# PEER gate weights built once at full width, half of them kept in DRAM; modulation rows split over two layers; one-hot sums of the MoE on VectorE

## The chip, the core and the metric

The kernel runs on one core of a Trainium2 chip. A core has TensorE for matrix multiplies (PE in the profile; its weight loads are PEld), VectorE (DVE), ScalarE (ACT), GpSimd (POOL) and SyncE (SP), which here only issues transfers. Engines run their own instructions in order and wait for each other through semaphores. SBUF is the on-chip memory of 128 partitions, PSUM the accumulators of TensorE, DRAM the large memory outside. The metric is the time of one execution in microseconds (us).

## The reference

Two transformer blocks in a row on 256 tokens of width 1024. The first has two layers of attention and a PEER feed-forward; the second has recurrent mixers and a mixture of experts (MoE) with 64 experts. The change touches three parts of it:

```python
# PEER, per token: 8 heads pick 16 of 128 x 128 experts each
top_s, pos = lax.top_k(cand, PEER_TOPK)
eidx = jnp.take_along_axis(cidx, pos, axis=-1)
g = jax.nn.softmax(top_s, axis=-1)
a = gelu(einsum('chkd,cd->chk', u[eidx], xc))
w = g * a
out = einsum('chk,chkd->cd', w, v[eidx])
...
# second block, before its layer: 6 modulation rows from a vector c
m = silu(c) @ w_mod[:, : 6 * D_MODEL] + b_mod
...
# MoE: 8 of 64 experts per token
sel = lax.top_k(cand, TOP_K)[1]
```

## The kernel before, in words

The kernel does not gather PEER's experts. It computes `u` times all tokens for all 128 x 128 experts, applies Gelu, multiplies by a dense gate array that is zero where an expert wasn't picked, and multiplies by all of `v`. `peer` does this for each layer `l` in four stages. An expert's number has two parts of 7 bits; a step `s` holds two values of the second part, each with 128 experts on the partitions.

- **First u half**, `ustep(0..31)`: each step loads two slots of `in_u` (512 KB each, tiles `rawA` and `rawB`), splits each into a high and a low part (`whi` by ACT, L280, `wlo` by DVE, L284), and runs 48 matmuls of 256 columns (three for each of 8 x 2 pieces). ACT applies Gelu into `WA`. Routing runs beside it.
- **Second u half**, `ustep(32..63)`: the same into `WB`. Beside it run 32 `gstep(g0, 0)`, one for 8 tokens each, which build the gates of `WA`.
- **First v half**, `vstep(0..31)`: each step splits two rows of `WA` into `hh` and `hl`, loads two slots of `in_v` and runs 24 matmuls of 512 columns into `acc`. Beside it run 32 `gstep(g0, 1)`, which build the gates of `WB`.
- **Second v half**, `vstep(32..61)` and `vlast`: the same on `WB`. In layer 0 there are beside it 48 `mod_step`: each loads 512 KB of `in_wmod` into the same `raw` tiles and DVE multiplies and sums it (L910).

A `gstep` makes one-hot matrices of 8 tokens by comparing with a row 0..127. `o1` (L739) compares with the first part of the expert's number, `oa` (L741) with the second part, 64 of the 128 values at a time; `ob` and `oa` are then multiplied by the low and the high part of the gate (L743, L744). The element order is (pair of token groups, value, token), with 4 tokens innermost and 16-bit elements. 16 matmuls `o1` x `oa` and `o1` x `ob` of 64 columns give the gates of 8 tokens in one PSUM tile `ps`, and DVE multiplies them into `W` (L751). So `o1` is built twice for each token, once per half. The tiles of a gstep lie in `a.raw` (`hr` in the profile), in two buffers that take turns.

`interleave(main, side)` writes the side steps between the main ones, each after the last `wlo` of the step before it (`issue_after(self.pin)`). The scheduler of the language then fixes the order on each engine. PSUM tiles alternate between tags `psA` and `psB`, two buffers each; `raw`, `whi` and `wlo` have two buffers per tag A and B, so two steps of weights are in SBUF at a time. `in_u`, `in_v` and `in_wmod` are all issued from SP, in order.

In the MoE, `onehot(q4)` builds for 4 experts two comparisons on DVE (L1643), then their sum `O` on POOL (L1644; for the first group on DVE) and its copy in bf16 `Ob` on POOL (L1645). `gather` uses `O` as the moving operand, `slots` uses `Ob`. POOL also computes the low part of every second down weight (`xlo`, L284).

Of the kernel before, what the change touches and what calls it, by code (L numbers as in the profile page):

```python
# [214 lines left out]
class K:  # L215
# [493 lines left out]
    def peer(self, l, a):  # L709
        nc, I, tc = self.nc, self.I, self.tc  # L710
        H = NK // 2
        with ExitStack() as es:
# [19 lines left out]
            def gstep(g0, hf):  # L732
                def f():
                    tk = lambda x: x[:, g0:g0 + 8].rearrange("p (g t) -> p g t", g=2).unsqueeze(2)
                    k = (g0 // 8) % 2
                    buf = a.raw[:, 4 * k:4 * k + 4, :].rearrange("p a n -> p (a n)").bitcast(F16)
                    o1 = buf[:, 0:1024].rearrange("p (g n t) -> p g n t", g=2, t=4)
                    oa, ob = [buf[:, 1024 + 512 * i:1536 + 512 * i].rearrange("p (g n t) -> p g n t", g=2, t=4) for i in range(2)]
                    nc.vector.tensor_tensor(o1, self.iota4.unsqueeze(1).broadcast_to([P, 2, 128, 4]),  # L739
                                            tk(idx[0]).broadcast_to([P, 2, 128, 4]), op=OP.is_equal)  # L740
                    nc.vector.tensor_tensor(oa, self.iota4[:, hf * H:(hf + 1) * H].unsqueeze(1).broadcast_to([P, 2, H, 4]),  # L741
                                            tk(idx[1]).broadcast_to([P, 2, H, 4]), op=OP.is_equal)
                    nc.vector.tensor_tensor(ob, oa, tk(idx[3]).broadcast_to([P, 2, H, 4]), op=OP.mult)  # L743
                    nc.vector.tensor_tensor(oa, oa, tk(idx[2]).broadcast_to([P, 2, H, 4]), op=OP.mult)  # L744
                    ps = self.ps()
                    for i in range(8):
                        o = ps[:, i * H:(i + 1) * H]
                        self.mm(o, o1[:, i // 4, :, i % 4], oa[:, i // 4, :, i % 4], i == 0, False)
                        self.mm(o, o1[:, i // 4, :, i % 4], ob[:, i // 4, :, i % 4], False, i == 7)
# [1209 lines left out]
```

## Time and profile before

| | |
|---|---|
| median of 3 runs | 3294.72 us (3287.04 to 3298.88) |
| the profiled execution | 3290.99 us |
| its span of instructions | 3289.2 us |
| PE busy | 3101.9 us, 94% |
| DVE busy | 2505.5 us, 76% |
| ACT busy | 1587.2 us, 48% |
| POOL busy | 512.5 us, 16% |
| mean DMA rate | 185 GB/s |

The difference between span and execution, 1.8 us, lies around the instructions. A busy PE is not PE at its peak: matmuls overlap, so their rate is read from the distance of their starts.

### The profile page before, as it was taken

How to read it: one execution, taken by the hardware profiler on the slowest of the kernel's cores; microseconds unless marked ns; L12 is line 12 of the kernel's file. 1: busy time of each engine (PE TensorE's matmuls, PEld its weight loads, DVE VectorE, ACT ScalarE, POOL GpSimd, SP SyncE). 2: the span in 40 equal slices, each digit the busy share in tenths (PEclk: the TensorE clock that was granted, in tenths of full speed). 3: DMA queues.
4: the chain of work that ended last, by engine and by line, in shares of the span. 5: the costliest groups of instructions: out<-in, count | busy, mean ns of one | idle time of the engine just before them, and what ended most of it. 6: DMA issues, size and time to landing. Idle time of an engine off the chain costs nothing. (4 is left out here: it accounts for less than half of the span.)

```text
span 3289.2 us, 53389 instructions
## 1 busy us (share of the span) xinstructions
PE 3101.9 (94%) x20908; PEld 2778.7 (84%) x20908; DVE 2505.5 (76%) x4367; ACT 1587.2 (48%) x2136; POOL 512.5 (16%) x278
## 2 busy tenths in 40 slices
PE   5999999999999899999999999979998899999997
PEld 5889999998876688999999888868897777877776
DVE  7655997778877776599777885566868888888886
ACT  4544443343344434444334334443244676667665
POOL 2010220000000323122000000010332332232221
PEclk8999999999999899999999999989998999999999
DMA  6335554445588521555544555642223678877875
GB/s 241 112 103 180 180 176 159 155 159 161 162 279 299 209 65 46 180 179 178 164 154 157 163 161 180 195 166 96 90 96 122 247 285 292 286 276 282 292 277 187
DMA packets 166726, 607.84 MB, mean 185 GB/s; under 512 B 18752, under 2 KB 19264, under 8 KB 165824
## 3 DMA queue, kind: packets, MB, share of 16 engines
q1 hardware_dynamic: 166464, 604.33, 54.3%
q8 instruction: 166, 2.72, 0.3%
q14 instruction: 96, 0.79, 0.1%
HBM read 600.57 MB, written 3.69 MB: 184 GB/s over the span
## 5 line engine op out<-in xcount | busy, mean ns | idle before, releaser
L280 ACT CAST whiA<-rawA 128x1024 fp32r<-128x1024 f32 (+1 forms) x439 | 460.4, 1049 | 582.3 <-PE psA L253 247.7
L280 ACT CAST whiB<-rawB 128x1024 fp32r<-128x1024 f32 (+1 forms) x449 | 471.3, 1050 | 531.6 <-PE psA L253 191.4
L284 DVE TENSOR_TENSOR wloA<-rawA,whiA 128x1024 fp32r<-128x1024 f32 x406 | 530.6, 1307 | 151.3 <-ACT whiA L280 148.4
L284 DVE TENSOR_TENSOR wloB<-rawB,whiB 128x1024 fp32r<-128x1024 f32 x421 | 528.8, 1256 | 129.6 <-ACT whiB L280 127.8
L253 PE MATMUL psA<-hh,whiA 128*128 128x256 f32 (+1 forms) x1096 | 322.2, 294 | 5.4 <-ACT hh L293 5.4
L253 PE MATMUL psA<-hl,whiA 128*128 128x256 f32 (+1 forms) x1096 | 316.4, 289 | 3.5 <-DVE hl L294 3.5
L253 PE MATMUL psA<-hh,wloA 128*128 128x256 f32 (+1 forms) x1096 | 316.0, 288 | 0.8 <-DVE wloA L284 0.7
L284 POOL TENSOR_TENSOR xlo<-xraw,xhi 128x1024 fp32r<-128x1024 f32 x64 | 164.3, 2568 | 484.4 <-ACT xhi L280 484.4
L253 PE MATMUL psA<-hh,whiB 128*128 128x256 f32 x832 | 238.1, 286 | 0.5 <-ACT hh L293 0.5
L253 PE MATMUL psA<-hl,whiB 128*128 128x256 f32 x832 | 235.4, 283 | 2.3 <-DVE hl L294 2.3
L253 PE MATMUL psA<-hh,wloB 128*128 128x256 f32 x832 | 235.4, 283 | 0.7 <-DVE wloB L284 0.7
L284 POOL TENSOR_TENSOR wloB<-rawB,whiB 128x1024 fp32r<-128x1024 f32 x28 | 74.5, 2662 | 985.3 <-ACT whiB L280 985.3
L284 POOL TENSOR_TENSOR wloA<-rawA,whiA 128x1024 fp32r<-128x1024 f32 x33 | 86.0, 2608 | 911.6 <-ACT whiA L280 846.4
L253 PEld LDWEIGHTS psA<-hh,whiA 128*128 128x128 f32 (+1 forms) x1096 | 216.2, 197 | 7.5 <-ACT hh L293 6.4
L253 PEld LDWEIGHTS psA<-hl,whiA 128*128 128x128 f32 (+1 forms) x1096 | 215.5, 197 | 5.7 <-issue 1.9
L253 PEld LDWEIGHTS psA<-hh,wloA 128*128 128x128 f32 (+1 forms) x1096 | 215.1, 196 | 1.7 <-DVE wloA L284 1.4
L253 PE MATMUL acc<-whiA,hh 128*128 128x512 f32 x512 | 199.2, 398 | 7.7 <-ACT whiA L280 5.8
L253 PE MATMUL acc<-wloA,hh 128*128 128x512 f32 x512 | 201.1, 393 | 4.9 <-DVE wloA L284 4.3
L253 PE MATMUL acc<-whiB,hh 128*128 128x512 f32 x512 | 202.2, 396 | 2.1 <-ACT hh L293 1.9
L253 PE MATMUL acc<-wloB,hh 128*128 128x512 f32 x512 | 199.8, 390 | 0.8 <-DVE wloB L284 0.8
L253 PE MATMUL acc<-whiA,hl 128*128 128x512 f32 x512 | 199.3, 390 | 0.0
L253 PE MATMUL acc<-whiB,hl 128*128 128x512 f32 x512 | 199.2, 390 | 0.0
(835 smaller groups left out, 8364.9 us busy)
## 6 DMA issues: line engine op xcount, KB each, us to landing
rawA<-in_moegu SPq DMA_DIRECT2D x130, 512.0 KB, 5.4
rawB<-in_moegu SPq DMA_DIRECT2D x130, 512.0 KB, 5.2
rawA<-in_u SPq DMA_DIRECT2D x128, 512.0 KB, 3.5
rawB<-in_u SPq DMA_DIRECT2D x128, 512.0 KB, 3.5
rawA<-in_v SPq DMA_DIRECT2D x128, 512.0 KB, 3.6
rawB<-in_v SPq DMA_DIRECT2D x128, 512.0 KB, 3.5
xraw<-in_moed SPq DMA_DIRECT2D x128, 512.0 KB, 5.8
rawB<-in_wt SPq DMA_DIRECT2D x40, 512.0 KB, 3.5
```

The lines of the kernel that those rows point to most:

```text
L253: self.pe = self.nc.tensor.matmul(out, lhsT, rhs, start=start, stop=stop, skip_group_check=True).ins
L280: self.nc.scalar.copy(hi[:, :n], w[:, :n])
L284: i = (eng or self.nc.vector).tensor_tensor(lo[:, :n], w[:, :n], hi[:, :n].bitcast(F32), op=OP.subtract)
```

## The change

- **Gates.** `gstep` now makes all 128 values of the second part at once: `oa` and `ob` are twice as wide, `o1` is built once, and a gstep has 16 matmuls of 128 columns into two PSUM tiles. So there are 32 gsteps per layer where there were 64. All of them run in the second u half, beside `ustep(32..61)`. DVE multiplies the first 64 values into `WA` at once, in two pieces. The other 64 are for rows of `WB` that Gelu hasn't written yet: ACT copies them out of PSUM (`late`), POOL writes them to a DRAM array `dgate` (256 KB per gstep), and in the first v half SP loads them back (`gload`, four ahead) and DVE multiplies them into `WB` (`gate`).
- The innermost dimension of the one-hots has 2 tokens (`iota2`) where it had 4.
- The buffers of the gsteps are `a.raw` (8 KB of it) and, for odd steps below `GT` = 28, the end of `WB`, which Gelu writes last.
- **Modulation.** 24 of the 48 `mod_step` run in the second v half of each layer.
- **One-hot sums.** `O` and `Ob` are both computed on DVE from the two comparisons; POOL has no part in `onehot`.

```diff
+GT = 28
...
-        self.iota4 = self.t(self.cp, [128, 4], "iota4", F16)
+        self.iota2 = self.t(self.cp, [128, 2], "iota2", F16)
...
-            def gstep(g0, hf):
+            def gstep(g):
                 def f():
...
+                    buf = raw if g % 2 == 0 or g >= GT else W[1].rearrange("p i t -> p (i t)")[:, 2 * GT * S:]
+                    o1, oa, ob = [buf[:, 512 * i:512 * i + 512].bitcast(F16).rearrange("p (g n t) -> p g n t", g=4, t=2) for i in range(3)]
+                    io = self.iota2.unsqueeze(1).broadcast_to([P, 4, NK, 2])
+                    nc.vector.tensor_tensor(o1, io, tk(idx[0]), op=OP.is_equal)
+                    nc.vector.tensor_tensor(oa, io, tk(idx[1]), op=OP.is_equal)
+                    nc.vector.tensor_tensor(ob, oa, tk(idx[3]), op=OP.mult)
+                    nc.vector.tensor_tensor(oa, oa, tk(idx[2]), op=OP.mult)
+                    late = buf[:, 1536:2048]
+                    for h in range(2):
+                        ps = self.ps()
+                        for i in range(4):
+                            o = ps[:, i * NK:(i + 1) * NK]
+                            gi, ti = 2 * h + i // 2, i % 2
+                            self.mm(o, o1[:, gi, :, ti], oa[:, gi, :, ti], i == 0, False)
+                            self.mm(o, o1[:, gi, :, ti], ob[:, gi, :, ti], False, i == 3)
...
+                        nc.vector.scalar_tensor_tensor(W[0][:, :, ts], W[0][:, :, ts], 2.0 ** -12, pv[:, 0:H, :], op0=OP.mult, op1=OP.mult)
+                        nc.scalar.activation(late.rearrange("p (i t) -> p i t", t=8)[:, :, 4 * h:4 * h + 4], pv[:, H:, :], AF.Identity, scale=2.0 ** -12)
+                    nc.gpsimd.dma_start(self.dgate[:, 512 * g:512 * g + 512], late)
...
+            def gload(g):
+                nc.sync.dma_start(raw[:, g % 4 * 512:g % 4 * 512 + 512], self.dgate[:, 512 * g:512 * g + 512])
+            def gate(g):
+                def f():
+                    Ws = W[1][:, :, 8 * g:8 * g + 8]
+                    nc.vector.tensor_tensor(Ws, Ws, raw[:, g % 4 * 512:g % 4 * 512 + 512].rearrange("p (i t) -> p i t", t=8), op=OP.mult)
+                    if g + 4 < S // 8:
+                        gload(g + 4)
...
-            self.interleave([ustep(s) for s in range(H // 2, H)], [gstep(g, 0) for g in range(0, S, 8)])
-            self.interleave([vstep(s) for s in range(H // 2)], [gstep(g, 1) for g in range(0, S, 8)])
...
+            self.interleave([ustep(s) for s in range(H // 2, H - 2)], [gstep(g) for g in range(S // 8)])
+            for s in range(H - 2, H):
+                ustep(s)()
+            vstep(0)()
+            for g in range(4):
+                gload(g)
+            self.interleave([vstep(s) for s in range(1, H // 2 - 2)], [gate(g) for g in range(S // 8)])
...
+            rest = [lambda: self.silu_row(cb, 2)] + [lambda j=j: self.mod_step(cb, j, junk) for j in range(24 * l, 24 * l + 24)]
+            if l == L - 1:
+                rest.append(self.mod_end)
...
-                eng.tensor_tensor(O, eq[0], eq[1], op=OP.add)
-                nc.gpsimd.tensor_copy(Ob, O.bitcast(F32))
+                nc.vector.tensor_tensor(O, eq[0], eq[1], op=OP.add)
+                nc.vector.tensor_tensor(Ob, eq[0], eq[1], op=OP.add)
```

**Where the instructions stand, first place: the end of the second u half of layer 0, on DVE.** `hr` is `a.raw`, `iota` the row to compare with, `idx` the expert numbers and gates of the tokens, `ps` a gstep's gates. Before, the last two gsteps on `WA` stand like this:

```order
L284 TENSOR_TENSOR wloB_7957<-rawB_7954,whiB_7956 128x1024
L739 TENSOR_TENSOR hr_74<-iota_12_86,idx_423_2419 128x1024
L741 TENSOR_TENSOR hr_74<-iota_12_86,idx_424_2420 128x512
L743 TENSOR_TENSOR hr_74<-hr_74,idx_426_2422 128x512
L744 TENSOR_TENSOR hr_74<-hr_74,idx_425_2421 128x512
L284 TENSOR_TENSOR wloA_8012<-rawA_8009,whiA_8011 128x1024
L751 SCALAR_TENSOR_TENSOR WA_2415<-WA_2415,psB_7905 128x64x8
L284 TENSOR_TENSOR wloB_8030<-rawB_8027,whiB_8029 128x1024
```

In the change, this is how the last two gsteps, 30 and 31, stand:

```order
L285 TENSOR_TENSOR wloA_8110<-rawA_8107,whiA_8109 128x1024
L756 SCALAR_TENSOR_TENSOR WA_2416<-WA_2416,psA_7994 128x64x4
L285 TENSOR_TENSOR wloB_8140<-rawB_8137,whiB_8139 128x1024
L756 SCALAR_TENSOR_TENSOR WA_2416<-WA_2416,psB_8005 128x64x4
L742 TENSOR_TENSOR hr_75<-iota_13_87,idx_424_2420 128x1024
L743 TENSOR_TENSOR hr_75<-iota_13_87,idx_425_2421 128x1024
L744 TENSOR_TENSOR hr_75<-hr_75,idx_427_2423 128x1024
L745 TENSOR_TENSOR hr_75<-hr_75,idx_426_2422 128x1024
L756 SCALAR_TENSOR_TENSOR WA_2416<-WA_2416,psA_8021 128x64x4
L756 SCALAR_TENSOR_TENSOR WA_2416<-WA_2416,psB_8032 128x64x4
```

The four vector operations of gstep 31 (L742 to L745) stand behind both products of gstep 30 (`psA_7994` and `psB_8005`), and on PE the matmuls of 30 and 31 follow each other with no ustep between them. In the rest of the stage the order is as before, with two products (L756) for one (L751).

**Second place: the start of the first v half, on SP**, the queue that issues the loads. Before:

```order
L265 DMA rawA_8009<-in_v 128x1024
L265 DMA rawB_8027<-in_v 128x1024
L265 DMA rawA_8069<-in_v 128x1024
L265 DMA rawB_8087<-in_v 128x1024
L265 DMA rawA_8129<-in_v 128x1024
L265 DMA rawB_8147<-in_v 128x1024
```

In the change:

```order
L266 DMA rawA_8212<-in_v 128x1024
L266 DMA rawB_8230<-in_v 128x1024
L762 DMA hr_75<-dgate_71 128x512 x4
L266 DMA rawA_8252<-in_v 128x1024
L266 DMA rawB_8270<-in_v 128x1024
L266 DMA rawA_8292<-in_v 128x1024
L266 DMA rawB_8310<-in_v 128x1024
L762 DMA hr_75<-dgate_71 128x512
L266 DMA rawA_8332<-in_v 128x1024
L266 DMA rawB_8350<-in_v 128x1024
```

The pair 8212 and 8230 is step 1, 8252 and 8270 step 2, and so on. Four `gload` stand between steps 1 and 2; `gload(4)` stands behind the loads of step 3, and from there one follows every step.

**Third place: the same stretch on DVE.** Before, a step of the first v half carries a whole gstep:

```order
L284 TENSOR_TENSOR wloA_8252<-rawA_8249,whiA_8251 128x1024
L294 TENSOR_TENSOR hl_76<-WA_2415,hh_75 128x512
L751 SCALAR_TENSOR_TENSOR WB_5298<-WB_5298,psA_8169 128x64x8
L284 TENSOR_TENSOR wloB_8270<-rawB_8267,whiB_8269 128x1024
L739 TENSOR_TENSOR hr_74<-iota_12_86,idx_423_2419 128x1024
L741 TENSOR_TENSOR hr_74<-iota_12_86,idx_424_2420 128x512
L743 TENSOR_TENSOR hr_74<-hr_74,idx_426_2422 128x512
L744 TENSOR_TENSOR hr_74<-hr_74,idx_425_2421 128x512
```

In the change:

```order
L285 TENSOR_TENSOR wloB_8233<-rawB_8230,whiB_8232 128x1024
L768 TENSOR_TENSOR WB_5299<-WB_5299,hr_75 128x64x8
L295 TENSOR_TENSOR hl_77<-WA_2416,hh_76 128x512
L285 TENSOR_TENSOR wloA_8255<-rawA_8252,whiA_8254 128x1024
L295 TENSOR_TENSOR hl_77<-WA_2416,hh_76 128x512
L285 TENSOR_TENSOR wloB_8273<-rawB_8270,whiB_8272 128x1024
L768 TENSOR_TENSOR WB_5299<-WB_5299,hr_75 128x64x8
```

`gate(0)` (the first L768) stands behind the last `wlo` of step 1 and ahead of those of step 2; one `gate` follows every step.

## Rows read from the trace of the kernel before

**Rows 1.** Stretches: the stages of layer 0, of layer 1, and one MoE period.

```profile
core 0: us, PE busy (x) PEld busy (x) DVE busy (x) ACT busy (x) POOL busy (x), PEclk, DMA share, GB/s
482.00:700.00 218.00, 218.00 (x2061) 216.57 (x2059) 157.74 (x234) 83.96 (x99) 0.00 (x0) 1.00 0.50 161
700.00:909.00 209.00, 208.04 (x1267) 171.24 (x1264) 171.59 (x252) 86.16 (x98) 0.00 (x0) 1.00 0.52 163
909.00:1106.00 197.00, 184.41 (x768) 141.84 (x769) 154.25 (x206) 81.98 (x95) 1.11 (x1) 1.00 0.87 294
1776.00:1985.50 209.50, 208.10 (x1267) 171.26 (x1265) 172.08 (x253) 84.40 (x97) 0.00 (x0) 1.00 0.51 161
1985.50:2160.50 175.00, 174.38 (x768) 144.06 (x768) 102.64 (x107) 82.86 (x95) 3.06 (x2) 1.00 0.59 190
2600.00:2644.00 44.00, 43.08 (x223) 35.71 (x223) 38.13 (x46) 32.28 (x44) 13.86 (x7) 1.00 0.78 288
```

**Rows 2.** PE's timeline, second u half: start, duration, instruction.

```profile
602.61 0.28 PE L253 MATMUL psA<-hh,wloB 128*128 128x256 f32 x1
602.73 1.16 PE L253 MATMUL psB<-hr 128*128 128x64 f16 x16
603.70 0.36 PE L253 MATMUL psA<-hh,whiA 128*128 128x256 f32 x1
603.90 0.28 PE L253 MATMUL psA<-hl,whiA 128*128 128x256 f32 x1
```

**Rows 3.** DVE's timeline, same stretch, one period and the start of the next.

```profile
603.93 0.69 DVE L751 SCALAR_TENSOR_TENSOR WA<-WA,psB 128x512 f32<-128x512 f32 x1 [1.69 <-PE psB L253]
604.53 1.22 DVE L284 TENSOR_TENSOR wloB<-rawB,whiB 128x1024 fp32r<-128x1024 f32 x1
605.67 0.69 DVE L739 TENSOR_TENSOR hr<-iota,idx 128x1024 f16<-128x1024 f16 x1
606.27 0.42 DVE L741 TENSOR_TENSOR hr<-iota,idx 128x512 f16<-128x512 f16 x1
...
610.74 0.69 DVE L751 SCALAR_TENSOR_TENSOR WA<-WA,psB 128x512 f32<-128x512 f32 x1 [1.70 <-PE psB L253]
```

**Rows 4.** DVE's groups by line and shape: count, busy us, mean ns.

```profile
L1697 DVE SCALAR_TENSOR_TENSOR msl<-msl,wc,psB 128x256 f32<-128x256 f32 x33 | 15.7, 475 | 3.3 <-ACT msl L1696 3.3
...
L1643 DVE TENSOR_TENSOR Oeq<-i,p 128x512 f16<-128x512 f16 x32 | 21.5, 683 | 0.7 <-POOL O L1644 0.7
```

**Rows 5.** Who waited for whom in the second v half of layer 0: us, times, longest.

```profile
ACT whiA L280 <- DMA rawA<-in_v: 33.0, 11, 5.0
...
PEld acc L253 <- DVE wloA L284: 11.4, 17, 1.1
PEld acc L253 <- ACT whiA L280: 10.9, 12, 1.6
```

**Rows 6.** DMA issues of the page: KB each, us from issue to landing.

```profile
rawB<-in_v SPq DMA_DIRECT2D x128, 512.0 KB, 3.5
```

**Rows 7.** The costliest groups of the page: count, busy us, mean ns, idle before.

```profile
L280 ACT CAST whiA<-rawA 128x1024 fp32r<-128x1024 f32 (+1 forms) x439 | 460.4, 1049 | 582.3 <-PE psA L253 247.7
```

**Rows 8.** MoE timeline of DVE, POOL and PE around one slow `wlo`.

```profile
2687.29 3.02 DVE L284 TENSOR_TENSOR wloA<-rawA,whiA 128x1024 fp32r<-128x1024 f32 x1 [0.32 <-ACT whiA L280]
2690.24 0.47 DVE L1697 SCALAR_TENSOR_TENSOR msl<-msl,wc,psA 128x256 f32<-128x256 f32 x1
...
2686.39 2.84 POOL L284 TENSOR_TENSOR xlo<-xraw,xhi 128x1024 fp32r<-128x1024 f32 x1 [3.97 <-ACT xhi L280]
2689.20 2.13 POOL L1644 TENSOR_TENSOR O<-Oeq,Oeq 128x512 fp32r<-128x512 f16 x1
...
2690.76 0.29 PE L253 MATMUL psA<-cb,Ob 128*128 128x2 bf16 x6 [1.44 <-DVE msl L1697]
```

**Rows 9.** The one-hot sums by line: duration ns min/median/max.

```profile
L1644 DVE TENSOR_TENSOR O<-Oeq,Oeq x1: 678/678/678, 2550.4 to 2550.4; 128x512 fp32r<-128x512 f16 x1
L1645 POOL CAST Ob<-O x16: 602/609/1632, 2551.2 to 3157.4; 128x512 bf16<-128x512 f32 x16
```

More of the change, by code (lines that the diff above doesn't have):

```diff
@@ L730, in ustep @@
                 return f
-            def gstep(g0, hf):
+            def gstep(g):
                 def f():
[L734 to L749, printed above, removed]
-                    Ws = W[hf][:, :, g0:g0 + 8]
-                    nc.vector.scalar_tensor_tensor(Ws, Ws, 2.0 ** -12, ps.rearrange("p (t i) -> p i t", t=8), op0=OP.mult, op1=OP.mult)
@@ new lines, in f @@
+                    g0 = 8 * g
+                    tk = lambda x: x[:, g0:g0 + 8].rearrange("p (g t) -> p g t", g=4).unsqueeze(2).broadcast_to([P, 4, NK, 2])
+                    buf = raw if g % 2 == 0 or g >= GT else W[1].rearrange("p i t -> p (i t)")[:, 2 * GT * S:]
+                    o1, oa, ob = [buf[:, 512 * i:512 * i + 512].bitcast(F16).rearrange("p (g n t) -> p g n t", g=4, t=2) for i in range(3)]
+                    io = self.iota2.unsqueeze(1).broadcast_to([P, 4, NK, 2])
+                    nc.vector.tensor_tensor(o1, io, tk(idx[0]), op=OP.is_equal)
@@ new lines, in f @@
+                    nc.gpsimd.dma_start(self.dgate[:, 512 * g:512 * g + 512], late)
+                return f
+            def gload(g):
[6 more added lines that the diff above has]
+                        gload(g + 4)
@@ L788, in peer @@
             acc += self.residual(a)
-            self.interleave([ustep(s) for s in range(H // 2, H)], [gstep(g, 0) for g in range(0, S, 8)])
-            self.interleave([vstep(s) for s in range(H // 2)], [gstep(g, 1) for g in range(0, S, 8)])
-            rest = []
-            if l == 0:
-                cb, junk = a.raw[:, 0:4, :].rearrange("p a n -> p (a n)"), a.raw[:, 4:8, :].rearrange("p a n -> p (a n)")
-                rest = [lambda: self.silu_row(cb, 2)] + [lambda j=j: self.mod_step(cb, j, junk) for j in range(48)] + [self.mod_end]
+            raw = a.raw.rearrange("p a n -> p (a n)")
+            self.interleave([ustep(s) for s in range(H // 2, H - 2)], [gstep(g) for g in range(S // 8)])
[5 more added lines that the diff above has]
+            self.interleave([vstep(s) for s in range(1, H // 2 - 2)], [gate(g) for g in range(S // 8)])
+            for s in range(H // 2 - 2, H // 2):
+                vstep(s)()
+            cb, junk = a.raw[:, 0:4, :].rearrange("p a n -> p (a n)"), a.raw[:, 4:8, :].rearrange("p a n -> p (a n)")
+            rest = [lambda: self.silu_row(cb, 2)] + [lambda j=j: self.mod_step(cb, j, junk) for j in range(24 * l, 24 * l + 24)]
+            if l == L - 1:
+                rest.append(self.mod_end)
             self.interleave([vstep(s) for s in range(H // 2, H - 2)] + [vlast], rest)
@@ L1634, in moe, with onehot @@
             nc.vector.tensor_copy(p16, p1)
-            def onehot(q4, eng=nc.gpsimd):
+            def onehot(q4):
                 O = self.t(pool, [NT, 2, P], "O", F32R, bufs=2)
@@ L1732, in scatter @@
                             self.mm(acc[t][q], ot[p][:, t * P:(t + 1) * P], y, False, p == npair - 1 and y is py[p][q][1])
-            onehot(0, nc.vector)
+            onehot(0)
             for c2 in range(4):
@@ L1830, in build @@
         self.dfeat, self.dret, self.dgdn = dram("dfeat", self.CS), dram("dret", 1024), dram("dgdn", 1024)
+        self.dgate = dram("dgate", S // 8 * 512)
         hq = ExitStack()
```

4 lines of the change are left out of this document (3 added, 1 removed).

## Prediction, made before the changed kernel was run

> **What bounds the kernel now.** I first cut the span into the stages that the change touches and read for each which engine is full [rows 1]. The second u half (482 to 700 us in layer 0) has PE busy for all of its 218.0 us. Its period is 6.81 us (from one L751 at 603.93 to the next at 610.74 [rows 3]; 218.0 / 32 = 6.81). The timeline of PE takes it apart [rows 2]: matmuls of a ustep start 0.12 us apart, so 48 take 5.76; the 16 gate matmuls run from 602.73 to 603.70, 61 ns each, and the matmul behind them takes 0.20 instead of 0.12. A gstep so costs PE 1.05 us, and 5.76 + 1.05 = 6.81. DVE waits 1.69 us in each period for PE's gate matmuls [rows 3]. So PE is the bound, and its clock is fully granted there (1.00 [rows 1]).
>
> The second v half of layer 1 is v work alone: 768 matmuls in 174.38 us, 0.227 each, 5.45 for a step. The first v half takes 209.0 and 209.5, 6.53 a step [rows 1], which is 5.45 plus 1.05 and a little: PE-bound too, and a sixth of it is gates.
>
> The second v half of layer 0 differs: 197.0 us with PE busy for 184.4, DMA share 0.87 and 294 GB/s [rows 1]. ACT waits there for loads of `in_v`, up to 5.0 us at a time, and PE's weight loads wait behind it for `whi` and `wlo` [rows 5]. This half is bound by loads: 64 slots of v and 48 of modulation, 197.0 / 112 = 1.76 us each.
>
> A MoE period of 4 experts has 44.0 us with PE at 43.1 and DVE at 38.1 [rows 1]: PE again, with one wait of 1.44 us [rows 8].
>
> **First v half: gates gone from PE.** Both v halves then have the same 768 matmuls, 174.4 us. 209.0 - 174.4 = 34.6 and 209.5 - 174.4 = 35.1: **-70 us**. What must stay hidden in a step of 5.45: on DVE two `wlo` of 1.14 each (604.53 to 605.67 [rows 3]), `hl` and the new `gate` of 512 elements each, 0.60 each by the 512-element L751 (603.93 to 604.53 [rows 3]); 3.5 in all. On ACT two `whi` of 1.05 [rows 7] and `hh`, under 3.2. Loads: two of 512 KB and one of 256 KB, 1.31 MB in 5.45 us or 241 GB/s, under the 294 that rows 1 show. On SP the `gload` waits for `gate(k)`, and the loads of step k+4 are queued behind it. But these loads wait anyway for a free `raw` buffer, that is for `wlo` of step k+2, and on DVE that stands behind `gate(k)`. So the new wait ends first, and I cost it at nothing; what it costs if that is wrong is a rival below.
>
> **Second u half: wider gates on PE.** Still 16 matmuls per gstep and 32 gsteps, now of 128 columns. The trace has 61 ns at 64 columns, 120 at 256 [rows 2] and 227 at 512 [rows 1]. From 256 to 512 it is 0.42 ns a column with 13 ns on top, which gives 67 at 128 (and 40 at 64, so something other than columns sets the 61). A straight line from 61 to 120 gives 81. I take 70, nearer the slope that the two long shapes agree on: 16 x 9 ns x 32 = 4.6 us a layer, **+9**; the bounds are +6 and +20. The Trainium skill (TensorE: Matmul & The Clock Gate, Back-to-back issue gap) gives about 81 ns between matmuls of 128 columns because weight loads and matmuls both set the distance. By that figure this term would be +20 and the sum 11 us less of a gain; its figure of 131 at 512 columns isn't what the rows here have (227), so I leave it at the upper bound.
>
> DVE must stay below PE's 6.95 per step. Its four operations of a gstep now have 1024 elements each. L739 has that size in the same 16-bit type and takes 0.60 from start to start (605.67 to 606.27 [rows 3]). The two products of 256 elements, one operand in PSUM, are like L1697 at 0.475 [rows 4], some 0.40 from start to start. 4 x 0.60 + 2 x 1.14 + 2 x 0.40 = 5.5, so 1.4 us are left and PE stays the bound. ACT is busy 84 of 218 us, 2.6 a step [rows 1]; two copies of 256 elements, each less than a `whi` of 1.05, leave it under 4.7. POOL is idle in this stage [rows 1] and has only the store to issue. A `late` buffer is used again two gsteps later, 13.6 us, so the store's length matters little until gstep 28.
>
> **The last two gsteps.** Gsteps 30 and 31 follow each other on PE, and from 28 on there is one buffer. DVE builds 31 only behind both products of 30, with a `wlo` between them: 0.40 + 1.14 + 0.40 + 4 x 0.60 = 4.3 us, of which PE's second half of gate 30 covers 0.5. PE waits about 4 us with nothing else queued: **+8** in two layers, bounds +5 and +12. The other doubled place (14 and 15) has two buffers, and 15 is ready. I find nothing late behind the stall: two usteps (11.5 us) and two vsteps lie between it and step 2, whose loads stand behind `gload(3)` and with it behind store 31.
>
> **Modulation in two halves.** Each half has 64 + 24 = 88 slots. At 1.76 each that is 155 us, under PE's 174.4, so PE becomes the bound in layer 0 and stays it in layer 1. DVE adds 1.3 us at most for a `mod_step` (a 1024-element operation like `wlo`) to less than 3.5 a step. Layer 0 gains 197.0 - 174.4 = 22.6, less 1.5 for steps in which loads bunch; layer 1 loses 1. **-20**, bounds -23 and -10.
>
> **One-hot sums.** DVE gets `O` (678 ns, the one time that DVE made it [rows 9]) and `Ob` (all operands 16-bit, 512 elements: 0.42 as L741 [rows 3]), 1.1 us per period; POOL loses 2.13 [rows 8] and 0.61 [rows 9]. DVE is idle for 44.0 - 38.1 = 5.9 us of a period, and the new rows stand where a comparison stood or ahead of its idle times. **0**. If all of it reached PE's path it would be 16 x 1.1 = +17; if the wait of 1.44 vanished, -23. I don't expect the latter: the `wlo` of 3.02 us that causes it (1.22 otherwise [rows 3]) started while POOL's `xlo` ran and ended after it [rows 8], and `xlo` stays on POOL.
>
> **Sum.** -70 + 9 + 8 - 20 + 0 = -73. The profiled execution took 3290.99, of which 3289.2 are span; 3291 - 73 = 3218. The median of the runs is 3.7 higher, 3294.7 - 73 = **3222**.
>
> **Rivals.**
> - *Pairs are slow on DVE.* With two tokens innermost the operations lose the fast rate. For it: the comparison L1643 with an operand that repeats innermost takes 683 ns for 512 elements of 16 bits [rows 4], L741 takes 420 for as many [rows 3]. Against: the change keeps two adjacent elements in every operand. No row has pairs. At the slow rate 1024 elements take as long as a `wlo`, 1.14 from start to start: 4 x 1.14 + 2.28 + 0.8 = 7.6 per step against 6.95 on PE, +0.7 x 32 = 22 a layer, and the stall grows by 2. 3222 + 48 = 3270. The Trainium skill (Vector Engine (DVE) Microarchitecture Reference, section 5.1) asks of the double rate only 16-bit operands, a step of one and more than one element innermost, and pairs meet that; by that rule this rival is out, and I give it 7 in 100.
> - *POOL's transfers stretch DVE.* If each of the 32 store issues holds up a DVE operation as `xlo` does, by 1.8 us [rows 8], DVE needs 7.3 of 6.95: +0.35 x 64 = 22, 3244. Against: one must fall on an operation that starts just then. The Trainium skill (SBUF — State Buffer, Who interferes with whom) has DVE operations with two SBUF inputs wait for GpSimd work that reads SBUF; that agrees with rows 8, but no run here shows a store issued by POOL. 8 in 100.
> - *Slower than before: SP stands still behind `gload`.* If the loads of a step could start only when the `gate` of the step before had run, each step would take issue and landing (0.7 + 3.5 [rows 6]), two `whi` (2.1), a `wlo` (1.2) and a `gate` (0.6), 8.1 us instead of 5.45: 2.65 x 29 x 2 = +154, 3376. It makes the change a loss from 6.7 us a step on. The order rows speak against it, with two steps of loads ahead. 5 in 100.
> - *The split doesn't help:* the 24 loads in layer 1 cost what layer 0 saves. Then 3242; 4 in 100. The rate of 1.76 per slot speaks against it.
>
> **How the numbers follow.** My sum has 76 in 100, by its bounds 3199 to 3243. 3222 is its time. The range 3196 to 3262 holds it, the POOL rival, the split and small moves in the MoE; it leaves out the slow pairs, the standing queue and what else might go wrong. A change within 0.3% (10 us) can't be told from none by these runs. Faster by more: all but the standing queue and some unforeseen case, 0.92; same 0.02; slower 0.06.
>
> **What would show it.** First v half: 174 to 176 us in both layers, no wait of PE for `whi`. Second u half: period 6.85 to 7.1, DVE still waiting for PE before each first product, L742 to L745 at 0.69 us (1.22 would be the first rival), one PE gap of about 4 us behind gate 30. Second v half: 175 to 178 us in both layers with DMA share under 0.8. MoE: still 44 us a period. The prediction is wrong if DVE never waits in the second u half, or if steps of the first v half exceed 5.6 us.

## The result

The changed kernel takes 3199.3 us (median of 4 runs, 3197.8 to 3200.4), the kernel before 3290.9 in the same series (4 runs, 3286.7 to 3298.9). The ratio is 0.972, with an interval of 0.9704 to 0.9736. The prediction of 3222 had the direction right and 18 us too little of a gain (it counted from 3294.7). The profiled execution took 3199.72 us, with a span of 3197.9; that is 91.3 less span than before.

To see where these 91 us lie, both traces are cut at the same events: first gate matmul, first matmul of the v work, the 769th (start of the second v half), the last, first gate of layer 1, and ACT's first and last `msl` of the MoE (`msl` is an expert's silu, which ACT makes and DVE multiplies).

| stretch, us | before | after | difference | predicted |
|---|---|---|---|---|
| second u half, layers 0 and 1 | 213.44, 213.39 | 215.95, 215.77 | +4.9 | +17 |
| first v half | 209.33, 209.35 | 174.11, 174.11 | -70.5 | -70 |
| second v half | 195.88, 173.99 | 174.35, 173.85 | -21.7 | -20 |
| end of layer 0's v to first gate of layer 1 | 457.46 | 464.17 | +6.7 | 0 |
| end of layer 1's v to the MoE | 405.59 | 400.90 | -4.7 | 0 |
| MoE | 698.84 | 692.65 | -6.2 | 0 |
| start and tail | 511.95 | 512.01 | +0.1 | 0 |

The windows of the changed kernel for these stretches, with the columns of [rows 1]; second u half, first and second v half of layer 0, start of layer 1, MoE:

```profile
486.41:702.36 215.95, 211.45 (x2002) 209.91 (x2001) 178.22 (x252) 103.12 (x160) 17.49 (x32) 0.99 0.59 198
702.36:876.47 174.11, 174.11 (x770) 144.16 (x769) 120.68 (x131) 86.80 (x101) 0.00 (x0) 1.00 0.74 238
876.47:1050.82 174.35, 174.14 (x768) 143.88 (x767) 127.20 (x152) 80.42 (x92) 2.38 (x1) 1.00 0.81 275
1050.82:1515.00 464.18, 430.58 (x3383) 412.73 (x3381) 354.19 (x857) 200.37 (x316) 120.51 (x73) 0.96 0.37 122
2479.62:3172.27 692.65, 664.24 (x3367) 549.85 (x3365) 591.84 (x713) 479.39 (x622) 170.50 (x65) 1.00 0.79 284
```

The same windows of the kernel before, where [rows 1] has none: second u half, start of layer 1, MoE.

```profile
487.13:700.57 213.44, 213.01 (x2019) 211.49 (x2017) 153.25 (x223) 82.78 (x97) 0.00 (x0) 1.00 0.49 159
1105.77:1563.23 457.46, 431.18 (x3382) 413.13 (x3381) 351.62 (x857) 199.61 (x316) 122.20 (x74) 0.97 0.39 130
2565.55:3264.39 698.84, 666.37 (x3367) 551.42 (x3365) 579.48 (x681) 478.85 (x623) 201.85 (x92) 0.99 0.78 282
```

In both v halves PE is busy for the whole of the stretch: they are matmuls and nothing else. In the second u half it isn't: 4.5 us are missing, and the clock's mean is 0.99.

PE's timeline of the changed kernel in the second u half, which answers to [rows 2]: start, duration, instruction.

```profile
595.26 0.28 PE L254 MATMUL psA<-hh,wloB 128*128 128x256 f32 x1
595.38 0.63 PE L254 MATMUL psB<-WB 128*128 128x128 f16 x8
595.86 0.62 PE L254 MATMUL psA<-WB 128*128 128x128 f16 x8
596.28 0.36 PE L254 MATMUL psB<-hh,whiA 128*128 128x256 f32 x1
596.48 0.28 PE L254 MATMUL psB<-hl,whiA 128*128 128x256 f32 x1
```

The 16 gate matmuls run from 595.38 to 596.28: 0.90 us, 56 ns each, although they have twice the columns of those before, which took 61. The period is 6.73 us (from 595.38 to the next at 602.12) where it was 6.81.

DVE's timeline in one period, which answers to [rows 3]:

```profile
602.79 0.42 DVE L756 SCALAR_TENSOR_TENSOR WA<-WA,psA 128x256 f32<-128x256 f32 x1 [0.90 <-PE psA L254]
...
604.79 0.69 DVE L742 TENSOR_TENSOR hr<-iota,idx 128x1024 f16<-128x1024 f16 x1
...
606.85 0.69 DVE L745 TENSOR_TENSOR hr<-hr,idx 128x1024 f16<-128x1024 f16 x1
...
609.52 0.42 DVE L756 SCALAR_TENSOR_TENSOR WA<-WA,psB 128x256 f32<-128x256 f32 x1 [0.85 <-PE psB L254]
```

The operations on pairs take 0.69 us, and DVE still waits 0.9 us for PE in each period: PE is the bound. POOL's 64 stores stretch none of them.

PE between gsteps 30 and 31, and then the granted clock (seventh column of a window) in the wait, 2 us behind it and 5 us behind it:

```profile
683.39 0.62 PE L254 MATMUL psB<-hr 128*128 128x128 f16 x8
688.34 0.64 PE L254 MATMUL psA<-hr 128*128 128x128 f16 x8 [4.34 <-DVE hr L745]
...
689.74 0.41 PE L254 MATMUL psA<-hl,whiA 128*128 128x256 f32 x1
689.95 0.41 PE L254 MATMUL psA<-hh,wloA 128*128 128x256 f32 x1
...
692.51 0.29 PE L254 MATMUL psA<-hh,wloA 128*128 128x256 f32 x1
692.64 0.29 PE L254 MATMUL psA<-hh,whiA 128*128 128x256 f32 x1
```

```profile
684.00:688.00 4.00, 0.01 (x1) 0.00 (x0) 3.86 (x7) 1.20 (x4) 0.54 (x1) 1.00 0.68 231
690.00:691.00 1.00, 1.00 (x6) 1.00 (x6) 0.08 (x1) 0.27 (x1) 0.00 (x0) 0.50 0.40 49
693.00:694.00 1.00, 1.00 (x11) 1.00 (x10) 0.00 (x0) 0.20 (x1) 0.00 (x0) 1.00 0.70 279
```

PE waits 4.34 us for gstep 31's one-hots, and then runs at the lower level (0.50, which is 1.2 GHz) until 692.5: matmuls start 0.21 us apart and not 0.12. The ustep behind the wait takes 7.22 us (689.38 to 696.60) in place of 5.84, so the clock adds some 1.3 us to the wait.

The kernel before had a wait of its own at this place, behind the gate matmuls of two gsteps, the second of which belongs to the next half:

```profile
697.97 1.16 PE L253 MATMUL psB<-hr 128*128 128x64 f16 x16
...
700.57 0.50 PE L253 MATMUL acc<-whiA,hh 128*128 128x512 f32 x1 [0.43 <-ACT hh L293]
```

SP's waits in the first v half of layer 0 (us in all, times, longest):

```profile
SPq L762 <- DVE WB L768: 6.5, 27, 0.3
SPq L762 <- DMA dgate<-hr: 3.3, 1, 3.3
```

A `gload` waits for `gate` at most 0.3 us; the single 3.3 us is `gload(3)` behind the last store. PE waits for neither.

At the start of layer 1, POOL's and then DVE's timeline of the changed kernel:

```profile
1052.53 2.34 POOL L285 TENSOR_TENSOR wloA<-rawA,whiA 128x1024 fp32r<-128x1024 f32 x1 [1.84 <-ACT whiA L281]
```

```profile
1051.36 1.28 DVE L442 BATCH_NORM_STATS2 bnst<-acc 128x6 f32<-128x512 f32 x2
1053.43 2.52 DVE L285 TENSOR_TENSOR wloB<-rawB,whiB 128x1024 fp32r<-128x1024 f32 x1 [0.80 <-ACT whiB L281]
1055.88 0.20 DVE L444 BATCH_NORM_AGGREGATE bnmv<-bnst 128x2 f32<-128x12 f32 x1
...
1058.04 0.80 DVE L467 TENSOR_SCALAR lnz<-acc,bnmv,zlnry 128x512 f32<-128x512 f32 x1
```

The `wlo` of a weight slot stands between the statistics of the second layer norm and its aggregate. It waits for `whiB` and is stretched from 1.22 to 2.52 us beside POOL's `wlo`, so `lnz` starts 7.2 us behind the end of the v work (1050.82); before, it was 3.1 us (behind 1105.77):

```profile
1108.86 0.80 DVE L466 TENSOR_SCALAR lnz<-acc,bnmv,zlnry 128x512 f32<-128x512 f32 x1
```

### The profile page after: what moved, and what is told of

Same layout as the page of the kernel before. It is cut to its first block, busy times and chain, and to the rows that moved or that the text cites. A ratio compares the mean times of both kernels' runs of the same rounds, so it can differ in the third digit from the quotient of the medians.

```text
span 3197.9 us, 51640 instructions
## 1 busy us (share of the span) xinstructions
PE 3012.0 (94%) x19884; PEld 2717.3 (85%) x19884; DVE 2466.8 (77%) x4206; ACT 1631.9 (51%) x2266; POOL 511.6 (16%) x311
## 3 DMA queue, kind: packets, MB, share of 16 engines
q8 instruction: 158, 2.59, 0.3%
## 5 line engine op out<-in xcount | busy, mean ns | idle before, releaser
L281 ACT CAST whiA<-rawA 128x1024 fp32r<-128x1024 f32 x423 | 443.6, 1049 | 453.0 <-PE psB L254 160.5
L281 ACT CAST whiB<-rawB 128x1024 fp32r<-128x1024 f32 x433 | 454.2, 1049 | 417.0 <-PE psB L254 178.7
L254 PE MATMUL psA<-hh,whiA 128*128 128x256 f32 x840 | 247.4, 294 | 5.5 <-ACT hh L294 5.5
L254 PE MATMUL psA<-hl,whiA 128*128 128x256 f32 x840 | 243.7, 290 | 2.7 <-DVE hl L295 2.6
L254 PE MATMUL psA<-hh,wloA 128*128 128x256 f32 x840 | 243.5, 290 | 2.1 <-DVE wloA L285 2.0
L254 PE MATMUL psB<-hh,wloB 128*128 128x256 f32 x832 | 238.6, 287 | 4.0 <-DVE wloB L285 4.0
L254 PE MATMUL psB<-hh,whiB 128*128 128x256 f32 x832 | 239.6, 288 | 0.0
L254 PE MATMUL psB<-hl,whiB 128*128 128x256 f32 x832 | 237.8, 286 | 0.0
L254 PEld LDWEIGHTS psA<-hh,whiA 128*128 128x128 f32 x840 | 166.4, 198 | 7.2 <-ACT hh L294 6.5
L254 PEld LDWEIGHTS psA<-hl,whiA 128*128 128x128 f32 x840 | 166.1, 198 | 4.3 <-POOL wloA L285 1.9
```

The lines of the kernel that those rows point to most:

```text
L254: self.pe = self.nc.tensor.matmul(out, lhsT, rhs, start=start, stop=stop, skip_group_check=True).ins
L281: self.nc.scalar.copy(hi[:, :n], w[:, :n])
```

## The experiments

All medians are set against the kernel before, run in the same series (3293.3, 3292.6 and 3291.4 in the three). Stage times are cut as above, of layer 0 where one is given.

| kernel | us | ratio, interval | second u | first v | second v | start of layer 1 | MoE |
|---|---|---|---|---|---|---|---|
| changed, again | 3203.1 | 0.9732, 0.9707 to 0.9757 | 216.6 | 174.1 | 173.9 | 461.4 | 693.2 |
| four tokens | 3259.2 | 0.9894, 0.9877 to 0.9911 | 244.0 | 174.1 | 173.9 | 464.2 | 696.9 |
| before, two tokens | 3231.4 | 0.9801, 0.9774 to 0.9828 | 198.3 | 194.9 | 196.9 | 461.8 | 698.3 |
| narrow | 3210.0 | 0.9751, 0.9738 to 0.9765 | 198.3 | 195.5 | 175.6 | 463.8 | 697.4 |
| spread | 3192.2 | 0.9692, 0.9675 to 0.9708 | 210.3 | 174.1 | 173.9 | 467.8 | 695.8 |
| modulation in layer 0 | 3225.5 | 0.9799, 0.9782 to 0.9815 | 216.5 | 174.1 | 199.0 | 459.3 | 691.4 |
| split 32 and 16 | 3203.3 | 0.9724, 0.9701 to 0.9746 | 215.9 | 174.1 | 173.9 | 460.2 | 709.2 |
| one-hot sums on POOL | 3210.2 | 0.9745, 0.9724 to 0.9767 | 216.5 | 174.1 | 174.0 | 464.3 | 701.6 |
| `xlo` on DVE | 3177.5 | 0.9651, 0.9628 to 0.9674 | 216.0 | 174.1 | 173.9 | 464.4 | 670.8 |
| `xlo` on DVE, sums on POOL | 3180.4 | 0.9665, 0.965 to 0.9679 | 216.6 | 174.1 | 173.9 | 461.4 | 672.7 |
| spread, `xlo` on DVE | 3165.3 | 0.9627, 0.9608 to 0.9645 | 210.3 | 174.1 | 174.0 | 463.8 | 668.2 |
| the same, split 32 and 16 | 3165.2 | 0.9616, 0.9602 to 0.9629 | 210.3 | 174.1 | 175.4 | 462.5 | 669.3 |

**What sets the time of a gate matmul.** The changed kernel with 4 tokens innermost:

```diff
...
-                    o1, oa, ob = [buf[:, 512 * i:512 * i + 512].bitcast(F16).rearrange("p (g n t) -> p g n t", g=4, t=2) for i in range(3)]
...
+                    o1, oa, ob = [buf[:, 512 * i:512 * i + 512].bitcast(F16).rearrange("p (g n t) -> p g n t", g=2, t=4) for i in range(3)]
...
-                            gi, ti = 2 * h + i // 2, i % 2
+                            gi, ti = h, i
```

> The one-hots of the changed kernel with 4 tokens innermost instead of 2, all else as changed: the matmuls still have 128 columns, but their operands have their elements 8 bytes apart instead of 4. Theory of the width: 16 gate matmuls take 0.90 us instead of the 0.97 before because they are wider or fewer per result; then the 0.90, the period of 6.73 us and 3199 stay. Rival, the distance of the elements: 16 matmuls take 0.97 again, the period is 6.80, and the time is 3199 + 2 x 32 x 0.07 = 3204. DVE's operations on pairs take 0.69 us, and by both they still take 0.69 here.

Both numbers were wrong. PE's and DVE's timelines:

```profile
618.47 1.12 PE L254 MATMUL psA<-hr 128*128 128x128 f16 x8
619.41 1.12 PE L254 MATMUL psB<-hr 128*128 128x128 f16 x8
620.28 0.37 PE L254 MATMUL psA<-hh,whiA 128*128 128x256 f32 x1
```

```profile
621.43 0.68 DVE L742 TENSOR_TENSOR hr<-iota,idx 128x1024 f16<-128x1024 f16 x1
```

The 16 matmuls take 1.81 us, twice the 0.90, and the kernel loses 60 us. DVE is as fast on fours as on pairs. So the distance of the elements counts, and more than either theory gave it. The kernel before with 2 tokens innermost, and nothing else changed:

```diff
...
-                    o1 = buf[:, 0:1024].rearrange("p (g n t) -> p g n t", g=2, t=4)
+                    o1 = buf[:, 0:1024].rearrange("p (g n t) -> p g n t", g=4, t=2)
...
-                        self.mm(o, o1[:, i // 4, :, i % 4], oa[:, i // 4, :, i % 4], i == 0, False)
+                        self.mm(o, o1[:, i // 2, :, i % 2], oa[:, i // 2, :, i % 2], i == 0, False)
...
```

> The kernel before with 2 tokens innermost in its one-hots instead of 4, all else as before: gate matmuls of 64 columns whose operands have their elements 4 bytes apart instead of 8. Known so far for 16 of them: 0.97 us for 64 columns at 8 bytes, 1.80 for 128 at 8 bytes, 0.90 for 128 at 4 bytes. Theory: the moving operand's distance sets the rate (0.81 ns a column at 8 bytes, half of it at 4), so 64 columns at 4 bytes need less than 0.90: about 0.5, unless the weight load sets a floor between 0.5 and 0.9. There are 128 such groups, all in stages bound by PE: 3293 goes to 3293 - 128 x (0.07 to 0.45), 3235 to 3284. Rival: the weights' distance sets the time of the 64-column matmuls; then 16 take 0.90 again, and the time is 3284. If they take 0.97, both are wrong.

```profile
504.99 0.65 PE L253 MATMUL psB<-hr 128*128 128x64 f16 x16
505.47 0.36 PE L253 MATMUL psA<-hh,whiA 128*128 128x256 f32 x1
```

16 take 0.49 us, 30 ns each. The four combinations are 61 and 113 ns for 64 and 128 columns at 8 bytes (0.81 ns for each added column), 30 and 56 at 4 bytes (0.40). All have 128 columns of weights, and at either distance the time nearly doubles with the columns of the moving operand alone; at 4 bytes no weight load sets a floor above 30 ns. The weights' distance changes together with the moving operand's in these runs, and no run changes one without the other; but the median record of a weight load goes from 97 to 117 ns only, whatever the width, so I put the halved rate down to the moving operand. The pairs alone make the kernel before 61 us faster. The Trainium skill (Advanced Engine Details and Errata, SBUF Cachelines) has full rate as long as at least two accesses hit the same 16 bytes; two elements 8 bytes apart do. For these matmuls the rows here disagree.

The whole change without the full width: `before, two tokens` with the modulation and the one-hot sums of the change; the gates are built in both halves. Of its edit, the part on the modulation:

```diff
...
-                rest = [lambda: self.silu_row(cb, 2)] + [lambda j=j: self.mod_step(cb, j, junk) for j in range(48)] + [self.mod_end]
...
+            rest = [lambda: self.silu_row(cb, 2)] + [lambda j=j: self.mod_step(cb, j, junk) for j in range(24 * l, 24 * l + 24)]
...
```

> The kernel before with 2 tokens innermost, the modulation split 24 and 24, and the one-hot sums on DVE: the whole change without the full width, that is, gates built 64 values at a time in both halves as before, and nothing through DRAM. Theory: the parts add up. With pairs at half width the second u half and the first v half took 198.3 + 194.5 = 392.8 us per layer, in the changed kernel they take 216.0 + 174.1 = 390.1; so this kernel is 5 to 6 us longer than the changed one, 3199 + 5.5 = 3205, and of the 91 us gained the full width and the way through DRAM hold no more than 6. Rival, the prediction's reading: the gates' leaving the v half is what gains most (70 us); then this kernel takes over 3240.

```profile
488.65:686.96 198.31, 197.26 (x2018) 195.81 (x2017) 153.22 (x223) 82.49 (x97) 0.00 (x0) 1.00 0.50 171
686.96:882.43 195.47, 192.68 (x1265) 156.51 (x1265) 169.16 (x253) 86.30 (x99) 0.00 (x0) 1.00 0.53 176
```

3210.0, 11 us over the changed kernel's first median and 7 over its second. 198.31 + 195.47 = 393.8 stands against 215.95 + 174.11 = 390.1 with the full width: 3.7 us a layer. The full width and the way through DRAM hold about 7 of the 91 us, near the theory's 6 and far from the prediction's reading. (Without the stall that the next run takes out they would hold more: there the two halves take 210.25 + 174.11 = 384.4.)

**The last two gsteps.** The second doubled place is moved:

```diff
-            self.interleave([ustep(s) for s in range(H // 2, H - 2)], [gstep(g) for g in range(S // 8)])
-            for s in range(H - 2, H):
-                ustep(s)()
+            k = 0
+            for s in range(H // 2, H):
+                ustep(s)()
+                for _ in range(1 + (s in (40, 50))):
+                    if k < S // 8:
+                        with self.tc.issue_after(self.pin):
+                            gstep(k)()
+                        k += 1
```

> The second doubled place of gsteps (30 and 31 behind each other, with one buffer) is moved to an earlier place where there are two buffers, so gstep 31 gets a ustep of its own. Theory: the stall at the end of the second u half costs the path 4.34 us of waiting and about 1.3 us in which PE then runs at half its clock, per layer, and a doubled place with two buffers costs 0.34; so each second u half gets shorter by 5.6 us and the time falls from 3199 to 3188. Rival: the stall covers something that ends later anyway (the loads of the first v steps stand behind the gload of gstep 3, and that behind the last store), so that PE waits at the start of the first v half instead; then each layer keeps 2 to 6 us of wait there and the time is 3195 to 3199.

```profile
485.74:695.99 210.25, 209.91 (x2003) 208.42 (x2001) 177.49 (x252) 103.00 (x160) 17.54 (x32) 1.00 0.57 201
```

The half is 5.7 and 5.5 us shorter, PE is busy throughout, the clock stays at 1.00 and the first v half stays at 174.1: nothing was hidden behind the stall. Of the 11 us, 7 show against the first median and as many as foreseen, 11, against the second. In the profiled execution (3197.9, the longest of four) the start of layer 1 and the stretch between layer 1's v work and the MoE were 4 us longer each than in the changed kernel's. The same edit is worth 12 beside the other edit that gained, at the end of this section (3177.5 with `xlo` on DVE alone, 3165.3 with both).

**Modulation.** All 48 steps in layer 0 again:

```diff
-            rest = [lambda: self.silu_row(cb, 2)] + [lambda j=j: self.mod_step(cb, j, junk) for j in range(24 * l, 24 * l + 24)]
...
+            if l == 0:
+                rest = [lambda: self.silu_row(cb, 2)] + [lambda j=j: self.mod_step(cb, j, junk) for j in range(48)] + [self.mod_end]
```

> Only the modulation goes back: all 48 steps beside the second v half of layer 0, none in layer 1. Both theories: that half goes from 174.4 back to 196, that of layer 1 stays at 174. They differ on the start of layer 1, where the changed kernel lost 6.5 us between the end of layer 0's v work and the first gates of layer 1. Theory: these belong to the split (with 24 steps the loads of the next weights come earlier, and DVE takes their low parts ahead of the layer norm), so they come back, and the time is 3199 + 22 - 6.5 = 3214. Rival: they belong to the order that the new gates bring, and stay; the time is 3221.

The time of 3225.5 is above both forecasts: the half takes 199.0 and not 196, for which I have no cause. The start of layer 1 goes back to 459.3; so part of the 6.7 us comes with the split, and the split is worth 22 to 26 us in medians. With 32 steps in layer 0, DVE's order has that `wlo` behind the layer norm:

```diff
-            rest = [lambda: self.silu_row(cb, 2)] + [lambda j=j: self.mod_step(cb, j, junk) for j in range(24 * l, 24 * l + 24)]
+            rest = [lambda: self.silu_row(cb, 2)] + [lambda j=j: self.mod_step(cb, j, junk) for j in (range(32) if l == 0 else range(32, 48))]
```

> The changed kernel with 32 of the 48 modulation steps in layer 0 and 16 in layer 1, instead of 24 and 24. In the order of DVE the low part of a weight slot of layer 1 then stands behind the second layer norm's vector work and not ahead of its aggregate. Theory: the start of layer 1 loses 5 to 7 us by that place alone, and 64 + 32 loads of 1.76 us each are 169 us, still under the 174 of PE; so the second v halves stay at 174, the stretch between layer 0's v work and the first gates of layer 1 goes from 464.2 back to 457 to 459.5, and the time from 3199 to 3193. Rival: it is the earlier end of the modulation loads, not the place in the order, and 32 steps give back only a part; the stretch stays at 462 to 464 and the time at 3197 to 3199. A third way: 32 steps are too many loads in the bunches, and the half in layer 0 grows to 178 or more; then 3200.

The second v half stays at 173.9, the start of layer 1 takes 460.2, but the time isn't shorter. In the profiled execution, 3212.75 and the longest of four, the MoE took 709.2, with the clock at 0.97 in two stretches of 100 us. The same step on a kernel with a steadier MoE:

> Both edits that gained, and 32 of the 48 modulation steps in layer 0 in place of 24. With the MoE steady, the 3 to 4 us can be seen that the stretch between layer 0's v work and the first gates of layer 1 should gain when DVE does the second layer norm ahead of a weight's low part. Theory: that stretch takes 457 to 461 us, and the time is 3162. Rival: the stretch moves by itself between 461 and 468 us, and the order of these two is not what sets it; then the time is that of the kernel with 24 steps, within 2 us.

462.5, and 3165.2 against 3165.3. The rival's time holds: with 24 steps this stretch took 461.4 to 467.8 in nine profiles, with 32 steps 460.2 and 462.5, with 48 457.5 to 461.8. By the means the split costs some 4 us there. But the edit with 32 steps didn't bring the layer norm ahead, so it doesn't test the theory. POOL's and DVE's timeline with 32 steps, where the v work ends at 1050.57:

```profile
1053.34 2.34 POOL L285 TENSOR_TENSOR wloA<-rawA,whiA 128x1024 fp32r<-128x1024 f32 x1 [2.43 <-ACT whiA L281]
1055.64 1.26 POOL L295 TENSOR_TENSOR hl<-hr,hh 128x512 fp32r<-128x512 f32 x1
```

```profile
1054.15 1.54 DVE L356 SCALAR_TENSOR_TENSOR zlnrt<-zlnry,zu 128x1 f32<-128x1 f32 x1
1055.73 1.19 DVE L361 SCALAR_TENSOR_TENSOR zlnry<-zlnrt,zlnry 128x1 f32<-128x1 f32 x1
...
1057.66 0.81 DVE L467 TENSOR_SCALAR lnz<-acc,bnmv,zlnry 128x512 f32<-128x512 f32 x1
```

Without the `wloB` two small operations of the norm are stretched, from 0.22 and 0.16 us, until POOL's `wloA` and `hl` end, and `lnz` still starts 7.1 us behind the v work: with 24 steps it is 7.2 in all nine profiles, with 48 it is 3.1 to 5.0. So the late layer norm can still be what the split costs; it isn't shown. The stretch also goes with the clock: its mean there is 0.97 in the two shortest (457.5 and 459.3) and 0.95 in the longest (467.8); which of the two causes the other stays open.

**MoE.** The sums back on POOL:

```diff
...
-                nc.vector.tensor_tensor(O, eq[0], eq[1], op=OP.add)
-                nc.vector.tensor_tensor(Ob, eq[0], eq[1], op=OP.add)
+                eng.tensor_tensor(O, eq[0], eq[1], op=OP.add)
+                nc.gpsimd.tensor_copy(Ob, O.bitcast(F32))
...
```

> Only the one-hot sums of the MoE go back to POOL, as in the kernel before; the gates and the modulation stay as changed. Theory: the 6.2 us that the MoE (from its first to its last silu) became shorter come from the move, because POOL's sums lay on other engines' path; then the MoE goes from 692.7 back to 698 to 700 and the time from 3199 to 3205. Rival, which is what the prediction said: the move is worth nothing and the 6 us are a matter of when loads land; then the MoE stays at 692 to 695 and the time at 3199 to 3201. Under both, PE's wait of 1.4 us for the msl once in 4 experts stays.

PE's longest wait of the MoE (us in all, times, longest) in the kernel before, the changed one and this one:

```profile
PE psA L253 <- DVE msl L1697: 27.6, 15, 4.3
```

```profile
PE psA L254 <- DVE msl L1725: 23.7, 15, 2.9
```

```profile
PE psA L254 <- DVE msl L1725: 27.9, 15, 2.6
```

The MoE takes 701.6, and the wait is back to what it was. All profiles with `xlo` on POOL say much the same: PE's waits for `msl`, those of both tags together, are 29.8 to 31.5 us in the three with the sums on POOL, and 24.2 to 29.6 in six of the seven with the sums on DVE (32.9 in the seventh, `split 32 and 16`); 3 to 4 us by the means. The medians differ by 7 to 11 us, but the intervals of the ratios overlap. To see how far the stages move by themselves:

> The changed kernel as it is, once more, to see how far its stages move from run to run. Theory: the stages that PE fills (both halves of u and v) repeat within 1 us; the MoE and the stretches of attention move by up to 4 us with the landing of loads and the clock; the time is 3195 to 3203. Rival: the MoE's 692.7 us were chance, and here it takes 697 or more, as it did in the kernel before.

693.2. With the sums on DVE the MoE took 691.4 to 697.4 in six profiles and 709.2 in one, with the sums on POOL 698.3 to 701.6 in three: likely shorter, by less than it moves by itself. Then the supposed cause of the wait, POOL's `xlo`, taken away:

```diff
-                    dw[e, f] = self.slot(I["moed"][1 + e, f], pool, nc.gpsimd if f else nc.vector)
+                    dw[e, f] = self.slot(I["moed"][1 + e, f], pool, nc.vector)
```

> The changed kernel with the low parts of all down weights of the MoE on DVE, where every second one was on POOL (64 of them). Theory: PE's wait for msl, 1.4 us once in 4 experts and 27 us in all, comes from the DVE operations that POOL's xlo stretches by some 1.5 us each (about 24 of them); without work on POOL they vanish, DVE is busy 592 + 64 x 1.22 - 41 = 629 of 670 us, and the MoE goes from 693 to some 668 and the time to 3175. Rival: DVE is so full then that PE waits for its wlo instead; at 94% busy and in a fixed order the waits grow, the MoE takes 690 to 710 and the time is 3197 to 3215.

The MoE window and PE's longest wait of this kernel, then one group of `wlo` (duration in ns, min/median/max) of the changed kernel and of this one:

```profile
2480.02:3150.84 670.82, 662.10 (x3367) 545.91 (x3365) 619.50 (x775) 479.58 (x623) 5.33 (x2) 1.00 0.82 293
```

```profile
PE psA L254 <- DVE msl L1725: 4.4, 5, 1.9
```

```profile
L285 DVE TENSOR_TENSOR wloB<-rawB,whiB x124: 1206/1219/3198, 2479.9 to 3162.5; 128x1024 fp32r<-128x1024 f32 x124
```

```profile
L285 DVE TENSOR_TENSOR wloB<-rawB,whiB x123: 1209/1218/1227, 2486.5 to 3143.0; 128x1024 fp32r<-128x1024 f32 x123
```

3177.5: the theory was right to 3 us. DVE takes over POOL's 64 operations and PE waits 19 us less; none of these `wlo` is stretched now. (One `wloA` of 2.96 us is left in this window; it starts beside one of the two operations that POOL still has there.) PE isn't at the lower clock level anywhere in this window, where it was for 3 to 24 us of it in the ten profiles with `xlo` on POOL. The Trainium skill (SBUF — State Buffer, Who interferes with whom) has DVE operations with two SBUF inputs wait for GpSimd work that reads SBUF, and the trace agrees: 3.2 us at most for these `wlo` with `xlo` on POOL, 1.23 without.

> The changed kernel with all low parts of the MoE's down weights on DVE, and the one-hot sums back on POOL, which now has nothing else to do there. Theory: POOL's sums stretch DVE operations that start while they run, so that PE's wait for msl comes back in part: some 0.45 us in each of 16 periods, as between the two kernels with xlo on POOL; the MoE goes from 671 to 678 and the time from 3177 to 3184. Rival: the sums mattered only because they stood in POOL's queue behind xlo; with POOL free they are early and nobody waits, and DVE has 1.1 us less to do per 4 experts; the MoE stays at 668 to 671.

MoE 672.7 against 670.8, time 3180.4 against 3177.5, between what the two had and with overlapping intervals: once `xlo` is off POOL, where the sums are made can hardly be measured.

**Both edits that gained:**

> The changed kernel with both edits that gained: the second doubled place of gsteps moved to where there are two buffers, and all low parts of the MoE's down weights on DVE. Theory: they lie in different stages and add up: 3177.5 - 11.4 = 3166. Rival: what the earlier start of the first v half gains is lost in the attention stretches that follow, as in the one profile with that edit alone, which were 3.6 and 4.1 us longer; then 3170 to 3177.

3165.3 us, as added up: 34 and 38 us under the changed kernel's medians, and 0.9627 (0.9608 to 0.9645) of the kernel before.

## Why the prediction was right, and where its sizes were off

- **First v half, -70.** Measured -70.5, PE busy throughout, SP's queue not held up. Right in size, but not as the reason of the gain: with the elements 8 bytes apart the v halves get shorter by the same 70.5 us, and the second u halves longer by 62 (four-token run, 244.0 and 244.8). What the gates' leaving is worth hangs on the next term.
- **Wider gates, +9.** This term was mis-sized, and it is the one to learn from. I priced 128 columns by a line through 256- and 512-column matmuls, whose elements are adjacent. [Rows 2] had the clue: 64 columns took 61 ns where the line gives 40, and I wrote that something other than columns sets it and passed on. It was the distance of the elements, which the change halves. Measured: 32 x (0.90 - 0.97) = -2.2 us a layer, -4.4 in all, outside my bounds of +6 and +20. With the distance kept, the four-token run has +28 us a layer in this half, and 56 to 60 of the 91 us would be gone. I had weighed the innermost pair for DVE alone, where it does nothing (0.69 us either way); it was an edit for PE, and by itself worth 61 us. The 81 ns of the Trainium skill (TensorE: Matmul & The Clock Gate, Back-to-back issue gap), my upper bound, fit neither 56 nor 113.
- **Last two gsteps, +8.** The wait was as said, 4.34 us, but it also costs 0.3 us to resume, 1.3 us of clock behind it, and 0.34 at the harmless doubled place: 12.5 us in two layers, just over my bound of +12. On the other side the second u half of the kernel before ended with a wait of its own (697.97 to 700.57: 32 gate matmuls in 2.59 us, not 1.94) and a gate of the next half (0.97), which went; I hadn't counted these -3.2. Together with the gates: -4.4 + 12.5 - 3.2 = +4.9, as measured.
- **Modulation, -20.** -21.7 in its stages; PE became the bound as said. I took what follows layer 0 to stay as it was; it got 6.7 us longer, some 4 of them with the split, by what way isn't settled.
- **One-hot sums, 0.** -6.2 in the profiled run; 3 to 4 us, by the means of ten profiles, are shorter waits of PE for `msl`, and the rest is within what this stage moves by itself. That the 1.44 us wait stays, with `xlo` on POOL as its cause, was right and is now shown.
- **The rivals** fell: pairs 0.69 us (the Trainium skill's rule on them, Vector Engine (DVE) Microarchitecture Reference, section 5.1, agrees), POOL's stores without effect, SP's wait 0.3 us a step, the split a gain.
- The 4.7 us between layer 1's v work and the MoE: the stretch took 404.6 to 405.6 in four profiles, two of them with the new gates and the split, and 399.7 to 401.7 in the other ten; no part of the change was shown to cause it.
- **Signs.** DVE waited for PE and no step of the v half exceeded 5.6 us, as said. The period of the second u half, 6.73, lies below the 6.85 to 7.1 that I named, and the DMA share of the second v half, 0.81, above 0.8.

So the 18 us that I missed are: second u half -12, MoE -6, that stretch -5, v halves -2, against +7 at the start of layer 1. The time lies 3 us inside the range of 3196 to 3262. That it lies there is in part luck: gates and stall each missed their own bounds, to opposite sides, and the sum's bounds of 3199 to 3243 had no working.

## What to carry to other kernels

- Price a matmul from a row with its own width *and* its own distance between elements; a row that lies off your line is a row to explain before the line is used.
- An edit that moves work and also changes its layout should be taken apart: here a change of layout was worth 61 us in the old kernel by itself, and the move 7 on top of it.
- Where PE waits, look for the engine pair behind it: moving 64 operations of the MoE from POOL, busy for 25% of it, to DVE, busy for 85%, gained 22 us, since the former had been stretching operations of the latter.
